# Matrix product with RMS norm on one core: a new order of steps, sums, squares and norms, and two row blocks loaded earlier

## The chip, the cores and the metric

The kernel runs on one core of one Trainium2 chip. The metric is the device time of one execution in microseconds (us). The kernel before has a median of 231.16 us over 3 runs (229.3 to 232.35). One further execution was profiled: it took 231.52 us, of which 229.7 us lie between its first and its last instruction (the span). All times of instructions below are counted from the start of that span.

A core has five engines that work side by side, each through its own queue in program order: PE (matrix products), DVE (vector work), ACT (activations, here squares, roots and copies), POOL (here almost only the loading of data) and SP (here only the issuing of output writes and of transposing transfers). They wait for each other through semaphores. Transfers between memories run on 16 DMA engines, which the loads from POOL and the transfers from SP share.

## The reference

```python
m, k, n = 2048, 2048, 2048          # a, b: randn float32; gamma: randn(n); eps = 1e-5
x = np.matmul(a, b)
rms = np.sqrt(np.mean(x ** 2, axis=-1, keepdims=True) + eps)
return (gamma * x / rms).astype(np.float32)
```

Every output row needs the whole row of x before it can be scaled, so squares are summed as chunks of the row come ready.

## The kernel before

**Tiling.** A has 16 row blocks of 128 rows (block 0 to 15), x has two column halves of 1024, each of two chunks of 512. Blocks 0 to 3 are the head; they are multiplied while B arrives. From block 4 on, two blocks make a group g (g = 2 to 7, rows `ra = 2g` and `rb = 2g + 1`). A group and a column half make a "half" n = 0 to 11, with g = 2 + n // 2 and j = n % 2.

**Products.** A half is computed as a 2 by 2 block product in Winograd's form of Strassen: seven products of 8 matmuls (128x512) each in place of eight. `do(n, m)` issues product m of half n and the copies of accumulators on ACT that belong to it; `take(n, what)` brings a finished chunk out (11 and 12 by ACT, 22 and 21 by an addition on DVE). `a_sums(g, which)` makes the sums of A's quarters on DVE that products 5, 6, 7 and 3 use. For groups 4 and 5, and for 6 and 7, product 2 (`a12*b21`) of the four halves together is replaced by a second level of the same scheme: `step(g, m, bank)` is one of its seven products of 4 matmuls; `a_two_sums(g)` makes its sums of A (in the tile x_5), `b_two(s)` those of B. Its results X2, W2 and Y2 (PSUM banks) are added into chunks of both groups by `add`.

**Row blocks of A.** A block is loaded as fp32 (1 MB) by POOL (`load_block`, L137) into one of two buffers of `a_pool`, so block m + 2 needs the buffer of block m. ACT takes its norm (`row_norm`, two squares and a root), DVE scales it to fp16 (`prepare`, L250, which calls `row_factor` and `row_apply`), and SP issues the transposing transfer into `at(m)` (L207 for blocks 6 to 9, L259 in two halves from block 10 on). A buffer of `a_pool` is free when both ACT's norm and DVE's scaling have read it. `at(m)` has four places: `at_even` and `at_odd`, two blocks each. `wait_for` is a POOL instruction that reads one element and so holds POOL's queue until that element is there; `load_after(src, mb)` is `wait_for(src)` and then `load_block(mb)`.

**Outputs.** `square_half` and `square_right` sum squares on ACT (the latter with the root); `finish` inverts on DVE, scales the two halves of a row block (2 x 1024 columns, gamma included) and lets SP write them.

**Order.** Every engine's order is written out by hand (`manual_schedule`): `first_segment` is n = 0; `segment(n)` is n = 1 to 9, of which n = 6 goes to `block_segment`; `last_group` is n = 10 and 11. Inside a segment the products of neighbouring halves alternate: half n's product 6, half n - 1's product 3, half n's product 2 (only before group 4), half n + 1's product 1, then n's products 7, 5 and 4. A PSUM bank that half n - 1 used (B3) must be read by `take(n - 1, 12)` or `take(n - 1, 22)` before the next product is put there.

**Where the blocks are loaded.** In the half with j = 1 of group g (`nxt = 2g + 2`), POOL waits for `at(nxt + 1)`, loads block nxt + 2, waits until it has landed and then loads nxt + 3 (L675, L676). So with g = 2 it is blocks 8 and 9, with g = 3 blocks 10 and 11, with g = 4 blocks 12 and 13, with g = 5 blocks 14 and 15. The norms of blocks 8 and 9 stand on ACT in segment n = 2 (L645 and L673).

Of the kernel before, what the change touches and what calls it, by code (L numbers as in the profile page):

```python
# [13 lines left out]
ALU = mybir.AluOpType  # L14
# [3 lines left out]
def kernel(  # L18
# [80 lines left out]
    def at(mb):  # L99
        return (at_even, at_odd)[(mb // 2) % 2][:, mb % 2]  # L100
# [4 lines left out]
    def add(out, in0, in1, op=ALU.add):  # L105
        nc.vector.tensor_tensor(out=out, in0=in0, in1=in1, op=op)  # L106
# [40 lines left out]
    def wait_for(src):  # L147
        nc.gpsimd.tensor_copy(out=pace, in_=src)
# [101 lines left out]
    def prepare(mb):  # L250
        row_factor(mb)
        if mb < 2 * (G2 + 1):
            row_apply(mb)
            transpose_dma(mb)
            return
        src, f = a32.pop(mb), factor.pop(mb)
        for h, dst in enumerate((a16_half, src.bitcast(FP16)[:, 0:HALF])):
            nc.vector.tensor_scalar_mul(out=dst, in0=src[:, h * HALF:(h + 1) * HALF], scalar1=f)
            nc.sync.dma_start_transpose(at(mb)[:, h * KP:(h + 1) * KP, :], dst)  # L259
# [24 lines left out]
    def square_half(mb, h):  # L284
        square_of(mb, x_tile(mb, h))
# [19 lines left out]
    def square_right(mb):  # L305

        square_half(mb, 1)
        rms_of[mb] = root(msq[mb][:, 2:3], pre_of.pop(mb))
# [28 lines left out]
    def a_sums(g, which, chained=True):  # L337
        a11, a12, a21, a22 = (quarter(g, r, c) for r in range(2) for c in range(2))
        terms = {3: (a22, sum_of(g, 2), ALU.subtract) if chained else (a11, a21, ALU.subtract),
                 1: (a21, a22, ALU.add),  # L340
                 2: (sum_of(g, 1), a11, ALU.subtract), 4: (a12, sum_of(g, 2), ALU.subtract)}
        for s in which:
            x, y, op = terms[s]
            nc.vector.tensor_tensor(out=sum_of(g, s), in0=x, in1=y, op=op)  # L344
# [45 lines left out]
    def a_two_sums(g):  # L390
        a11, a12, a21, a22 = (a_two(g, r, h) for r in range(2) for h in range(2))
        y1, y2, y3, y4 = (y_two[:, n] for n in range(4))
        add(y3, a11, a21, ALU.subtract)
        add(y1, a21, a22)
        add(y2, y1, a11, ALU.subtract)
        add(y4, a12, y2, ALU.subtract)
# [171 lines left out]
    def do(n, m, copies=True):  # L568

        if n >= len(halves) or n < 0:  # L570
            return
        g, j = halves[n]
        b1, b2, b3 = B1[n % 2], B2[n % 2], B3[n % 2]
        if g >= G2:
            b1 = b2
        product(g, j, m, {1: b1, 2: b1, 3: b3, 4: b2, 5: b3, 6: b2, 7: B7}[m],
                start=m in (1, 7))
        if m == 1 and g >= G2:
            nc.scalar.copy(out=chunks(n)[0], in_=b2)
        elif m == 1:  # L580
            nc.scalar.copy(out=b2, in_=b1)
        elif m == 6:
            nc.scalar.copy(out=b3, in_=b2)  # L583
        elif m == 7 and copies:
            nc.scalar.copy(out=chunks(n)[2], in_=B7)  # L585
# [13 lines left out]
    def load_after(src, mb):  # L599
        wait_for(src)  # L600
        load_block(mb)

    def first_segment():
        n, g, j = 0, G0, 0
        nxt = 2 * g + 2
        do(n, 1)
        do(n, 7, False)
        finish(0, (1,))
        pair_ends()
        do(n, 2)  # L610
        row_norm(nxt)
        a_sums(g, (4,))
        finish(0, (0,))
        do(n, 6)
        do(n + 1, 1)
        prepare(nxt)
        do(n, 5)
        nc.scalar.copy(out=chunks(n)[2], in_=B7)
        take(n, 22)
        row_norm(nxt + 1)  # L620
        take(n, 11)
        finish(1)
        do(n, 4)
        prepare(nxt + 1)
        take(n, 21)
        square_half(2 * g + 1, j)
# [7 lines left out]
    def segment(n):  # L634
        g, j = halves[n]
        ra, rb, nxt = 2 * g, 2 * g + 1, 2 * g + 2
        more = g + 1 < NG
        if g >= G2 and (g - G2) % 2 == 1 and j == 0:
            block_segment(n)
            return  # L640
        first = g >= G2 and (g - G2) % 2 == 0
        do(n, 6)
        if j == 0:
            finish(ra - 1)
            row_norm(nxt)  # L645
        elif g == G0:
            square_right(r2)
        do(n - 1, 3)
        take(n - 1, 12)
        if j == 0:  # L650
            square_right(ra - 2)
            prepare(nxt)
            a_sums(g, (4,))
            finish(ra - 2)
        else:
            if not first:
                square_half(ra, 0)
            if g == G0:
                square_right(r3)
                finish(r2, (1, 0))  # L660
            elif g == G2:
                b_two(4)
            elif not first and g > G2:
                finish(ra - 2)
        if g < G2:
            do(n, 2)
            take(n, 11)
        if g == G2 - 1 and j == 1:
            b_two(3)
            b_two(1)  # L670
        do(n + 1, 1)
        if j == 0:
            row_norm(nxt + 1)  # L673
        elif g + 2 < NG:
            load_after(at(nxt + 1)[:, KT - 1, 0:1], nxt + 2)  # L675
            load_after(a32[nxt + 2][:, 0:1], nxt + 3)  # L676
        if j == 1:
            a_sums(g + 1, (1, 2))
            if first:
                a_two_sums(g)  # L680
        do(n, 7)
        if j == 1:
            a_sums(g + 1, (3,))
        do(n, 5)
        take(n, 22)
        if j == 1:
            take_pre(rb)
            if not first:
                take_pre(ra)
        do(n, 4)  # L690
        take(n, 21)
        if j == 0:
            square_half(rb, 0)
            prepare(nxt + 1)
            if g == G2:
                b_two(2)
        else:
            square_right(rb)
            if g == G0:
                finish(r3, (1, 0))  # L700

    def block_segment(n):
        g, j = halves[n]
        ra, rb, nxt = 2 * g, 2 * g + 1, 2 * g + 2
        x00, x01, x10, x11 = first_sums(n)
        do(n, 6)
        finish(ra - 1)
        step(g - 1, 1, X2)
        nc.scalar.copy(out=W2, in_=X2)
        row_norm(nxt)  # L710
        do(n - 1, 3)
        step(g - 1, 2, W2)
        step(g - 1, 6, X2)
        nc.scalar.copy(out=Y2, in_=X2)
        take(n - 1, 12)
        add(x00, W2, x00)
        square_half(ra - 2, 0)
        prepare(nxt)
        do(n + 1, 1)
        step(g - 1, 5, Y2)  # L720
        step(g - 1, 7, W2)
        add(x11, Y2, x11)
        take_pre(ra - 2)
        row_norm(nxt + 1)
        a_sums(g, (4,))
        add(x10, W2, x10)
        add(x11, W2, x11)
        do(n, 7)
        step(g - 1, 4, X2)
        add(x10, X2, x10)  # L730
        do(n, 5)
        take(n, 22)
        step(g - 1, 3, Y2)
        add(x01, Y2, x01)
        square_right(ra - 2)
        prepare(nxt + 1)
        do(n, 4)
        take(n, 21)
        square_half(rb, 0)

    def last_group():
# [12 lines left out]
        def by_r(x, r):  # L754
# [2 lines left out]
        b2, b3 = [B2[(n + j) % 2] for j in range(2)], [B3[(n + j) % 2] for j in range(2)]  # L757
        x00, x01 = first_sums(n)[0:2]
        do(n, 6)
        finish(rb - 2)  # L760
        step(g - 1, 1, X2)
        nc.scalar.copy(out=W2, in_=X2)
        do(n - 1, 3)
        step(g - 1, 2, W2)
        step(g - 1, 6, X2)
        nc.scalar.copy(out=Y2, in_=X2)
        take(n - 1, 12)
        add(x00, W2, x00)
        square_half(ra - 2, 0)
        do(n + 1, 1)  # L770
        step(g - 1, 5, Y2)
        step(g - 1, 7, W2)
        add(x11[1], Y2, x11[1])
        take_pre(ra - 2)
        a_sums(g, (4,))
        add(x11[0], W2, x11[0])
        add(x11[1], W2, x11[1])
        square_of(ra, x11[1])
        do(n, 5)
        nc.scalar.copy(out=x22[0], in_=b3[0])  # L780
        step(g - 1, 4, X2)
        add(x11[0], X2, x11[0])
        do(n + 1, 6)
        step(g - 1, 3, Y2)
        add(x01, Y2, x01)
        square_right(ra - 2)
        do(n, 7)
        add(x22[0], x21[0], x22[0])
        add(b2[0], b2[0], x21[0])
        square_of(rb, x22[0])  # L790
        add(x11[1], x11[1], gam[2], ALU.mult)
        finish(ra - 2)
        do(n + 1, 5)
        nc.scalar.copy(out=x22[1], in_=b3[1])
        wide = a_pool.tile([P, K], FP32, name="a32")
# [4 lines left out]
        do(n, 3)  # L800
        take(n, 12)
        square_half(ra, 0)
        add(xa, xa, gam_left, ALU.mult)
        pre_a = stat_pool.tile([P, 1], FP32, name="pre")
        nc.vector.tensor_scalar(out=pre_a, in0=msq[ra][:, 0:1], scalar1=msq[ra][:, 1:2],
                                scalar2=msq[ra][:, 2:3], op0=ALU.add, op1=ALU.add)
        do(n + 1, 3)
        take(n + 1, 12)
        square_of(ra, x12[1])
# [84 lines left out]
```

## Time and profile before

| What | Value |
|---|---|
| Median of 3 runs | 231.16 us (229.3 to 232.35) |
| Profiled execution | 231.52 us, span 229.7 us |
| PE busy | 211.4 us, 92% of the span, 1004 matmuls |
| DVE busy | 161.7 us, 70% |
| ACT busy | 113.0 us, 49% |
| POOL busy | 37.0 us, 16% |
| Mean granted TensorE clock | 0.976 of full speed |
| Matmul 128x512, from one to the next, at full clock | 1.73 us for 8 |
| Load of a row block, issue to landing | 5.0 least, 5.4 median, 9.1 most (us, 10 loads) |
| Transposing transfer of a block (L207), issue to landing | 4.3 least, 4.3 median, 6.9 most (us, 4 transfers) |
| Output write of 512 KB, issue to landing | 3.6 median (us, 29 writes) |

How to read it: PE is busy for 92% of the span, and its 8% of pauses lie in a few places. A pause of PE counts fully if nothing that follows has slack to take it up. A row of the timeline gives the start, the busy time, the engine, the line of the code, the operation with its tiles, the number of instructions merged, and in brackets the idle time before it with the instruction that ended it. Matmuls overlap, so eight of them show 1.89 us busy though the next eight start 1.73 us later.

### The profile page before, as it was taken

How to read it: one execution, taken by the hardware profiler on the slowest of the kernel's cores; microseconds unless marked ns; L12 is line 12 of the kernel's file. 1: busy time of each engine (PE TensorE's matmuls, PEld its weight loads, DVE VectorE, ACT ScalarE, POOL GpSimd, SP SyncE). 2: the span in 40 equal slices, each digit the busy share in tenths (PEclk: the TensorE clock that was granted, in tenths of full speed). 3: DMA queues.
4: the chain of work that ended last, by engine and by line, in shares of the span. 5: the costliest groups of instructions: out<-in, count | busy, mean ns of one | idle time of the engine just before them, and what ended most of it. 6: DMA issues, size and time to landing. Idle time of an engine off the chain costs nothing.

```text
span 229.7 us, 2952 instructions
## 1 busy us (share of the span) xinstructions
PE 211.4 (92%) x1004; PEld 97.9 (43%) x1024; DVE 161.7 (70%) x323; ACT 113.0 (49%) x225; POOL 37.0 (16%) x74
## 2 busy tenths in 40 slices
PE   7999999999999999993799999999999999799960
PEld 3445454444454444441244444344444444344430
DVE  1237688999999858972853897687956956752981
ACT  2110004701987748574543972394738841445772
POOL 8544443342010002000011002100021000000030
PEclk9999999999999999999589999999999999999996
DMA  7999999999875695999254894488585972030255
GB/s 149 174 203 206 201 206 209 211 208 308 347 237 227 165 269 157 334 307 347 90 114 178 336 267 91 183 329 131 111 325 185 306 220 46 29 153 3 106 222 220
DMA packets 36911, 46.60 MB, mean 203 GB/s; under 512 B 22432, under 2 KB 26528, under 8 KB 35616
## 3 DMA queue, kind: packets, MB, share of 16 engines
q0 software_dynamic: 10608, 23.86, 42.8%
q1 hardware_dynamic: 26016, 22.29, 31.9%
q10 hardware_dynamic: 272, 0.26, 0.3%
q8 instruction: 8, 0.13, 0.2%
q14 instruction: 7, 0.06, 0.1%
HBM read 34.60 MB, written 16.78 MB: 224 GB/s over the span
## 4 chain that ended last, share of the span: by engine, by line
PE 33%; DVE 12%; DMA 7%; ACT 5%; issue 2%; SPq 1%; ACTq 0%; DVEq 0%
PE acc L367 28%; DVE x L106 5%; DMA a<-in_a_dram 4%; PE acc L406 3%; DVE x L320 3%; DMA head_at<-a 3%; DVE s L344 2%; ACT sq L281 2%; PE tbank L406 2%; ACT sq L229 1%; DVE head_at L344 1%; SPq L259 1%; DVE acc L106 1%; DVE a L106 1%; ACT rms L297 1%
## 5 line engine op out<-in xcount | busy, mean ns | idle before, releaser
L281 ACT ACTIVATE sq<-x 128x1024 bf16<-128x1024 f32 (+1 forms) x33 | 33.2, 1005 | 39.2 <-DVE x L106 35.9
L367 PEld LDWEIGHTS <-s 128*128 128x128 f16 (+1 forms) x312 | 30.7, 99 | 43.4 <-issue 7.3
L415 PE MATMUL acc<-b,head_at 128*128 128x512 bf16 x171 | 42.6, 380 | 0.2
L320 DVE SCALAR_TENSOR_TENSOR x<-x,r,gamma_sb 128x1024 f32<-128x1024 f32 x28 | 34.8, 1282 | 0.5
L367 PE MATMUL acc<-b,head_at 128*128 128x512 bf16 x133 | 34.8, 390 | 0.2
L106 DVE TENSOR_TENSOR x<-acc,x 128x512 f32<-128x512 f32 x33 | 22.6, 689 | 15.7 <-ACT x L585 5.1
L367 PE MATMUL acc<-b,s 128*128 128x512 bf16 x100 | 25.9, 399 | 5.2 <-DVE x L106 5.0
L229 ACT ACTIVATE sq<-a 128x1024 bf16<-128x1024 f32 x24 | 25.4, 1057 | 6.3 <-DMA a<-in_a_dram 5.9
L367 PEld LDWEIGHTS <-head_at 128*128 128x128 f16 (+1 forms) x184 | 18.2, 100 | 22.2 <-issue 2.2
L367 PE MATMUL acc<-b,at_even 128*128 128x512 bf16 x110 | 26.2, 379 | 0.2
L367 PE MATMUL acc<-early,s 128*128 128x512 bf16 x103 | 25.5, 379 | 0.1
L415 PEld LDWEIGHTS <-head_at 128*128 128x128 bf16 x176 | 17.0, 98 | 19.5 <-issue 0.9
L367 PEld LDWEIGHTS <-at_even 128*128 128x128 f16 x160 | 15.7, 98 | 18.9
L367 PE MATMUL acc<-t_left,s 128*128 128x512 bf16 x95 | 22.5, 379 | 0.0
L120 POOL DMA_DIRECT2D b<-in_b_dram x32 | 17.2, 540 | 20.6 <-DMA b<-in_b_dram 14.3
L451 ACT COPY x<-acc 128x512 f32<-128x512 f32 x7 | 4.1, 580 | 25.9 <-PE acc L415 25.9
L189 DVE COPY head_at<-tbank 128x1024 bf16<-128x1024 bf16 x7 | 4.8, 692 | 8.4 <-PE tbank L184 8.4
L106 DVE TENSOR_TENSOR x<-tbank,x 128x512 f32<-128x512 f32 x9 | 6.2, 692 | 4.8 <-PE tbank L441 3.6
L302 DVE RECIPROCAL r<-rms 128x1 f32<-128x1 f32 x16 | 2.5, 159 | 9.9 <-ACT rms L297 9.9
L820 POOL TENSOR_SCALAR x<-x,r 128x512 f32<-128x512 f32 x1 | 1.9, 1853 | 45.3 <-DVE r L302 45.3
L583 ACT COPY acc<-acc 128x512 f32<-128x512 f32 x12 | 6.9, 576 | 2.3 <-PE acc L367 2.3
L585 ACT COPY x<-acc 128x512 f32<-128x512 f32 x10 | 5.8, 576 | 4.6 <-PE acc L367 4.6
(129 smaller groups left out, 242.8 us busy)
## 6 DMA issues: line engine op xcount, KB each, us to landing
out_dram<-x SPq DMA_DIRECT2D x29, 512.0 KB, 3.6
a<-in_a_dram POOLq DMA_DIRECT2D x10, 1024.0 KB, 5.4
b<-in_b_dram POOLq DMA_DIRECT2D x32, 256.0 KB, 9.9
a<-in_a_dram POOLq DMA_DIRECT2D x4, 512.0 KB, 9.8
early<-in_a_dram POOLq DMA_DIRECT2D x7, 256.0 KB, 10.3
gamma_sb<-in_gamma_dram POOLq DMA_DIRECT2D x2, 512.0 KB, 9.9
out_dram<-x SPq DMA_DIRECT2D x3, 256.0 KB, 2.6
out_dram<-a SPq DMA_DIRECT2D x1, 768.0 KB, 3.3
```

What stands on the lines that cost most here:

```text
L106: nc.vector.tensor_tensor(out=out, in0=in0, in1=in1, op=op)
L120: nc.gpsimd.dma_start(out=raw[j][kp][:, t, :], in_=b[lo:lo + P, j * HALF:(j + 1) * HALF])
L189: nc.vector.tensor_copy(out=head_at[:, 2 * kp:2 * kp + 2, :, :], in_=view)
L229: nc.scalar.activation(out=junk, in_=a32[mb][:, h * HALF:(h + 1) * HALF], func=ACTF.Square, scale=2.0 ** -8, accum_out=n2[:, h:h + 1])
L281: nc.scalar.activation(out=sq[:, 0:src.shape[-1]], in_=src, func=ACTF.Square, scale=inv_sqrt_n, accum_out=msq[mb][:, c:c + 1])
L320: nc.vector.scalar_tensor_tensor(out=x, in0=x, scalar=inverse_of[mb], in1=gamma_sb[:, h * HALF:(h + 1) * HALF], op0=ALU.mult, op1=ALU.mult)
L344: nc.vector.tensor_tensor(out=sum_of(g, s), in0=x, in1=y, op=op)
L367: nc.tensor.matmul(bank, lhsT[:, kp, :], rhs, start=(start and kp == 0), stop=(kp == KP - 1), skip_group_check=not start)
L406: nc.tensor.matmul(bank, lhsT[:, k, :], rhs, start=(m in (1, 7) and k == 0), stop=(k == KQ - 1), skip_group_check=m not in (1, 7))
L415: nc.tensor.matmul(bank, head_at[:, kt, r, :], head_rhs(c, kt), start=(kt == 0), stop=(kt == KT - 1))
L583: nc.scalar.copy(out=b3, in_=b2)
L585: nc.scalar.copy(out=chunks(n)[2], in_=B7)
```

## The change

Two loads are moved forward: block 8 is loaded from `first_segment`, right after `prepare(6)`, and block 10 from segment n = 2, right after `prepare(8)`; POOL then waits for `at(7)` before block 9, and for `at(9)` before block 11. From group 4 on, loading is as before. In the j = 1 halves of groups 4 and 6 (n = 5 and 9), `a_two_sums` stands before `a_sums(g + 1, (1, 2))`, and `square_right(rb)` leaves the end of the segment: it now stands in `block_segment` and `last_group` behind the first copy of X2 to W2. In these two, `finish` of that row comes two steps later, step 4 is issued right behind step 7, step 3 before `do(n, 5)` in `block_segment`, norms and preparations of the next blocks come later, and in `last_group` some squares, one `finish` and one small sum of squares (`pre_a`) come in another order.

```diff
@@ first_segment
         prepare(nxt)
+        load_block(nxt + 2)
         do(n, 5)
@@ segment
         if j == 0:
             square_right(ra - 2)
             prepare(nxt)
+            if g < G2:
+                load_block(nxt + 2)
             a_sums(g, (4,))
             finish(ra - 2)
...
         elif g + 2 < NG:
-            load_after(at(nxt + 1)[:, KT - 1, 0:1], nxt + 2)
-            load_after(a32[nxt + 2][:, 0:1], nxt + 3)
+            wait_for(at(nxt + 1)[:, KT - 1, 0:1])
+            if g >= G2:
+                load_block(nxt + 2)
+                wait_for(a32[nxt + 2][:, 0:1])
+            load_block(nxt + 3)
         if j == 1:
-            a_sums(g + 1, (1, 2))
             if first:
                 a_two_sums(g)
+            a_sums(g + 1, (1, 2))
...
-            square_right(rb)
+            if not first:
+                square_right(rb)
@@ block_segment
         do(n, 6)
-        finish(ra - 1)
         step(g - 1, 1, X2)
         nc.scalar.copy(out=W2, in_=X2)
-        row_norm(nxt)
+        square_right(ra - 1)
         do(n - 1, 3)
         step(g - 1, 2, W2)
         step(g - 1, 6, X2)
         nc.scalar.copy(out=Y2, in_=X2)
+        finish(ra - 1)
         take(n - 1, 12)
         add(x00, W2, x00)
-        square_half(ra - 2, 0)
-        prepare(nxt)
         do(n + 1, 1)
         step(g - 1, 5, Y2)
         step(g - 1, 7, W2)
+        step(g - 1, 4, X2)
+        square_half(ra - 2, 0)
+        row_norm(nxt)
         add(x11, Y2, x11)
-        take_pre(ra - 2)
-        row_norm(nxt + 1)
         a_sums(g, (4,))
         add(x10, W2, x10)
         add(x11, W2, x11)
+        take_pre(ra - 2)
         do(n, 7)
-        step(g - 1, 4, X2)
+        row_norm(nxt + 1)
         add(x10, X2, x10)
+        prepare(nxt)
+        step(g - 1, 3, Y2)
         do(n, 5)
         take(n, 22)
-        step(g - 1, 3, Y2)
         add(x01, Y2, x01)
         square_right(ra - 2)
-        prepare(nxt + 1)
         do(n, 4)
         take(n, 21)
+        prepare(nxt + 1)
         square_half(rb, 0)
@@ last_group
         do(n, 6)
-        finish(rb - 2)
         step(g - 1, 1, X2)
         nc.scalar.copy(out=W2, in_=X2)
+        square_right(rb - 2)
         do(n - 1, 3)
         step(g - 1, 2, W2)
         step(g - 1, 6, X2)
         nc.scalar.copy(out=Y2, in_=X2)
+        finish(rb - 2)
         take(n - 1, 12)
         add(x00, W2, x00)
-        square_half(ra - 2, 0)
         do(n + 1, 1)
         step(g - 1, 5, Y2)
         step(g - 1, 7, W2)
+        step(g - 1, 4, X2)
+        square_half(ra - 2, 0)
         add(x11[1], Y2, x11[1])
-        take_pre(ra - 2)
         a_sums(g, (4,))
         add(x11[0], W2, x11[0])
         add(x11[1], W2, x11[1])
+        take_pre(ra - 2)
         square_of(ra, x11[1])
         do(n, 5)
         nc.scalar.copy(out=x22[0], in_=b3[0])
-        step(g - 1, 4, X2)
         add(x11[0], X2, x11[0])
-        do(n + 1, 6)
         step(g - 1, 3, Y2)
         add(x01, Y2, x01)
         square_right(ra - 2)
+        do(n + 1, 6)
+        finish(ra - 2)
         do(n, 7)
...
         add(x11[1], x11[1], gam[2], ALU.mult)
-        finish(ra - 2)
         do(n + 1, 5)
...
         square_half(ra, 0)
-        add(xa, xa, gam_left, ALU.mult)
         pre_a = stat_pool.tile([P, 1], FP32, name="pre")
         nc.vector.tensor_scalar(out=pre_a, in0=msq[ra][:, 0:1], scalar1=msq[ra][:, 1:2],
                                 scalar2=msq[ra][:, 2:3], op0=ALU.add, op1=ALU.add)
+        add(xa, xa, gam_left, ALU.mult)
```

Each engine executes as many instructions as before, except POOL, which has two waits (`wait_for`) fewer.

## The prediction

> **What bounds the kernel now.** I read the page's shares first: PE is busy for 92% of the span, no other engine for more than 70%. So only PE's pauses, and what follows its last matmul, can be won. The slices show where they lie: PE falls to 3 and 7 in slices 19 and 20, and PEclk, the granted clock, falls with it.
>
> ```profile
> PE   7999999999999999993799999999999999799960
> PEclk9999999999999999999589999999999999999996
> ```
>
> The timeline of PE gives the size of each pause (start, busy time, bracket: idle before and what ended it):
>
> ```profile
> 103.53 1.89 PE L367 MATMUL acc<-early,s 128*128 128x512 bf16 x8
> 110.42 3.57 PE L367 MATMUL acc<-b,s 128*128 128x512 bf16 x8 [5.00 <-DVE x L106]
> 113.78 3.08 PE L367 MATMUL acc<-b,head_at 128*128 128x512 bf16 x8
> 116.70 1.89 PE L367 MATMUL acc<-b,at_even 128*128 128x512 bf16 x8
> ...
> 146.92 1.89 PE L367 MATMUL acc<-b,s 128*128 128x512 bf16 x8
> 149.84 1.02 PE L406 MATMUL acc<-b,at_even 128*128 128x512 bf16 x4 [1.03 <-ACT acc L709]
> ...
> 195.94 1.89 PE L367 MATMUL acc<-b,s 128*128 128x512 bf16 x7
> 199.27 1.02 PE L406 MATMUL acc<-b,at_even 128*128 128x512 bf16 x4 [1.44 <-ACT acc L762]
> ```
>
> The big pause is followed by two products at half speed; the windows view shows the clock (after the five busy columns: PEclk, DMA share, GB/s):
>
> ```profile
> 109.00:111.00 2.00, 0.58 (x2) 0.25 (x2) 1.22 (x2) 0.64 (x2) 0.00 (x0) 0.59 0.57 231
> 111.00:113.00 2.00, 2.00 (x7) 0.65 (x5) 1.90 (x7) 1.63 (x3) 0.00 (x0) 0.50 0.00 0
> 113.00:115.00 2.00, 2.00 (x6) 0.67 (x5) 1.94 (x7) 0.94 (x2) 0.00 (x0) 0.50 0.36 72
> 115.00:117.00 2.00, 2.00 (x8) 0.81 (x7) 1.16 (x3) 0.89 (x3) 0.00 (x0) 0.70 1.03 191
> ```
>
> Last the chain of waits (start, length, what), read from the transfer down: block 9's load lands at 106.49, ACT takes its norm, only then copies B7 (L585), DVE does take(2, 22), and PE may write that bank.
>
> ```profile
> 97.36 9.13 DMA a<-in_a_dram
> 106.49 0.02 issue
> 106.51 1.16 ACT sq L229 x2
> ...
> 109.08 0.57 ACT x L585
> 109.65 0.02 issue
> 109.67 0.70 DVE x L106
> ```
>
> The same view leads the two pauses at 149.84 and 199.27 back through ACT's copies (L709, L762) to square_right of the row before: its squares and root stand before them in ACT's queue and wait for DVE's take(21), which is late because a_sums and a_two_sums start only when block 11 (or 15) is transposed (142.10, 191.53).
>
> **Early loads: the gain.** POOL's queue stands at its wait for at(7) from 66.9 to 87.4 us, so load 8 now goes out once DVE has scaled block 6, at 77.1 (before: 88.23). Block 9 needs only at(7) and goes out near 89 in place of 97.36; with the 9.13 us that load took among other traffic it lands by about 98. ACT reaches norm 9 earlier too: norm 8 starts behind the copy that ends at 95.0, not at 96.70, so norm 9 starts at about 100.5, B7 is copied by 103.6, take(2, 22) is done by 104.4. PE is ready at 103.53 + 1.73 = 105.26 (8 matmuls start 1.73 apart in every undisturbed row). So the pause of 110.42 - 105.26 = 5.16 us goes. With it goes the slow clock: 116.70 - 110.42 = 6.28 us for two products, 2.82 over 2 x 1.73. Together **-7.98 us**. Next late is take(2, 22) itself, with 0.9 us to spare.
>
> A rule bears on the second term. The row is 2.82 us. The Trainium skill (TensorE: Matmul & The Clock Gate, "What's actually happening") says that an idle window of about 3.4 us halves the clock and a busy one of 3.4 us restores it; an estimate from that page alone would be 1.7 us lost, and a sum 1.1 us smaller. I keep the row.
>
> **Early loads: the cost.** Load 8 now runs beside the transposing transfer of block 6 (issued 77.19) and the writes at 80.00. PE needs at(6) at 84.53, in product 1 of half 2. Rows: at(9), alone, landed 4.3 us after issue; at(8), with load 9 beside it for 5 us, 6.9 us, and SP was held for 4.82 us, not 1.93. By 4.3 at(6) lands at 81.5, by 6.9 at 84.1: no cost. If it had to wait for a whole load of 9.13 first, 77.19 + 9.13 + 4.3 = 90.6: 6.1 us of pause and 2.8 of slow clock. I take **+0.5**, near the 6.9 row, but load 8 lies beside all of it. SP's writes and at(7) slip behind; at(7) landed at 87.4 and PE needs its sums at 91.44, two DVE operations (1.5 us) after landing, so 2.5 us are covered. Load 10 meets at(8) likewise: prepare(8) ends near 100.2, 6.9 more is 107.1, PE needs it at 105.26 + 2 x 1.73 = 108.7: nothing, with 1.6 us to spare. Loads 10 and 11 are wanted by ACT 5 us or more after they land (ACT took norms 10 and 11 at 126.50 and 131.50, so some 8 us before that now). POOL's two dropped waits free only POOL.
>
> A rule of the Trainium skill speaks against this part: DMA: Bandwidth & Descriptors, "Queues, rings and completion order", has each DMA engine take turns between queues packet by packet. At half rate the alone row doubles to 8.6 us as an estimate, at(6) lands at 85.8, and the cost would be 1.3, not 0.5.
>
> **Steps, squares, norms.** Moving a_two_sums forward: it reads blocks 8 and 10 only, and DVE is idle for 1.21 us (4.65 at the second place) before block 11 (15) lands, so its 1.6 us end at about 142.6, and the sum for product 6 is ready at 144.1 where PE wants it at 144.33: 0.2 us to spare. Moving square_right behind the copy to W2: the copy is then ready at 147.5, and PE needs it at 146.92 + 1.73 = 148.65, so 149.84 - 148.65 = **-1.19 us**. Next late is step 7: finish now stands before add(x00, W2): root 149.2, reciprocal and two 1.28 us scalings to 151.9, addition to 152.5; PE comes to step 7 at 152.97. 0.4 us to spare; with step 4 behind it, the bank of step 3 is added long before.
>
> Norms and preparations of 12 and 13 come later. By ACT's and DVE's durations (a norm 2.56 us, a preparation 2.3) norm 12 ends at 156.5 and at(12) is issued near 159.6 instead of 155.50, landing about 162.9; PE wants it at 164.2: covered. at(13) lands 0.4 us later than its 167.1, hence loads 14 and 15 too: block 15 lands near 179.3 + 0.4 (issue 173.93 plus the median 5.4), while ACT, now 1.19 ahead, wants it at 180.17 - 1.19 = 179.0. That 0.7 us passes through L585, take(8, 22) and prepare(15) to at(15), which already was the last thing product 6 of half 10 waited for (193.15 against 193.01). I give back **+0.6**.
>
> In the last group three pauses go: 195.94 - 195.75 = 0.19, 199.27 - 197.67 = 1.60, and 220.57 - 219.99 = 0.58, before the last two half products, which waited for DVE. There finish of row 12 (2.48 us) and the multiplication of xa (1.2 us) stood before pre_a and the inverse (219.49); with finish done by 211 and pre_a first, the inverse comes near 216.7 and the bank additions by 217.7, PE being ready at 218.2. **-2.37 us**, if the tail behind it (root, last scalings, writes) moves whole.
>
> **Sum.** -7.98 + 0.5 - 1.19 + 0.6 - 2.37 = -10.44. The profiled execution took 231.52, 1.82 more than its span and 0.36 over the median: 231.52 - 10.44 = **221.1 us**.
>
> **Rivals.**
> - *Transposes held up*: each of at(6) and at(8) late by 1 to 2 us (twice the 4.3 row), at(7) and load 9 with them. For: DMA share is already 1.17 at 79 to 81 us. Against: at(8) beside load 9 came in 6.9. Price 2 to 4: 223 to 225.
> - *The new order gives nothing*: finish before step 7, or the late norms, make a pause as long as the one removed. For: only 0.2 and 0.4 us to spare. Against: each row computed above. Without the 0.6 and the 2.37: about 224.
> - *Slower*: a transfer of POOL's, once queued, is finished before the transposing one beside it. Then at(6) costs 6.1 + 2.8 = 8.9, and at(8), at 100.2 + 13.4 = 113.6 against 108.7, another 4.9 + 2.8: 16.6 against gains of 10.9, 231.5 + 5.7 = 237. It decides once at(6) and at(8) together cost more than 10.9. Against: behind load 9, at(8) landed at 108.3, not 106.49 + 4.3 = 110.8.
> - *Load 8 does not go earlier*: no, the order listing has it ahead of POOL's wait, and DVE's scaling of block 6 is its last condition. At most the steps' part would be left (-1.19 + 0.6 - 2.37): 228.6.
>
> **How the numbers follow.** Forecast 0.64, held transposes 0.18, order without gain 0.08, load not earlier 0.02, slower 0.05, and a mixture that eats all 0.03. Two per cent (4.6 us) is about what a measurement of this kernel tells from no change, so faster means below 226.5. Forecast and the first two rivals lie below it: 0.90; the fourth and the mixture between: 0.05; slower 0.05. Range: down to the gains without any give-back (231.5 - 11.5 = 220.0) less 1.2 for the spread of the runs, 218.8; up to the held transposes, 225.0.
>
> **What would show it.** Right: no pause of PE near 105, clock 1.00 there, load 8 out near 77, load 9 near 89, ACT not waiting for a transfer before norms 8 and 9; W2's copy (now L715, L769) before square_right, and no pause ahead of step 2. Wrong: a pause at product 1 of half 2 or 4 ended by a transposing transfer, a pause at step 7 ended by DVE, or product 6 of half 10 waiting longer for at(15).

## The result and the profile after

The changed kernel takes 238.51 us, the median of 4 runs (237.75 to 239.57). The kernel before took 231.28 us on the same chip (4 runs, 229.3 to 232.35). The ratio is 1.033 (95%: 1.024 to 1.041): slower, where 221.1 us had been forecast. The profiled execution took 237.75 us, with a span of 236.0 us and a mean granted clock of 0.959 (before: 0.976).

The slices of the page after, to be read against those of before:

```profile
PE   7799999999999931999999999999999579999970
PEclk9999999999999985799999999999999958999997
```

The hole of before in slices 19 and 20 is closed. In its place there is a larger one in slices 15 and 16, and a new one in slices 32 and 33, each with the slow clock behind it. The timeline of PE says what ended them (start, busy time, bracket: idle before and what ended it):

```profile
82.69 1.89 PE L367 MATMUL acc<-b,at_even 128*128 128x512 bf16 x8
93.39 3.59 PE L367 MATMUL acc<-b,head_at 128*128 128x512 bf16 x8 [8.82 <-DMA head_at<-head_at]
96.78 1.97 PE L367 MATMUL acc<-early,s 128*128 128x512 bf16 x8
98.59 1.89 PE L367 MATMUL acc<-b,at_even 128*128 128x512 bf16 x8
...
149.53 1.89 PE L367 MATMUL acc<-b,s 128*128 128x512 bf16 x8
151.25 1.03 PE L406 MATMUL acc<-b,at_even 128*128 128x512 bf16 x4
...
184.06 1.89 PE L367 MATMUL acc<-early,s 128*128 128x512 bf16 x8
190.18 2.29 PE L367 MATMUL acc<-b,s 128*128 128x512 bf16 x5 [4.23 <-DVE x L106]
...
196.45 1.89 PE L367 MATMUL acc<-early,s 128*128 128x512 bf16 x8
...
204.22 1.89 PE L367 MATMUL acc<-b,s 128*128 128x512 bf16 x7
205.95 1.03 PE L406 MATMUL acc<-b,at_even 128*128 128x512 bf16 x4
```

The first hole is product 1 of half 2, which waits for `at(6)`: 93.39 - (82.69 + 1.73) = 8.97 us of pause, and (98.59 - 93.39) - 2 x 1.73 = 1.74 us lost to the slow clock, **+10.71** together. The second is product 3 of half 8: 190.18 - (184.06 + 1.73) = 4.39 us, and (196.45 - 190.18) - 2 x 1.73 = 2.81 us, **+7.20**. No product between 98.59 and 190.18 shows a wait in its row: the 7.98 us of before near 105 are gone. The rows at 151.25 and 205.95 have no bracket any more, so the pauses ahead of step 2 are gone too.

The chain of waits names the transfers behind both holes (start, length, what):

```profile
77.06 16.28 DMA head_at<-head_at
...
171.54 5.26 DMA a<-in_a_dram
177.66 8.59 DMA a<-in_a_dram
186.28 1.16 ACT sq L229 x2
...
190.18 2.29 PE acc L367 x5
```

The transposing transfer of block 6 took 16.28 us where the same transfer took 4.3 alone. Block 15's load took 8.59 us where 5.5 had been enough before, and ACT's norm of block 15, with the copy of B7 behind it, stood until it landed.

The windows view shows what the DMA engines did in the first hole (after five busy columns: PEclk, DMA share, GB/s):

```profile
80.00:82.00 2.00, 2.00 (x11) 0.88 (x9) 1.90 (x6) 0.09 (x1) 0.00 (x0) 1.00 1.97 147
82.00:84.00 2.00, 2.00 (x11) 0.90 (x10) 1.54 (x2) 0.43 (x1) 0.00 (x0) 1.00 0.84 91
...
90.00:92.00 2.00, 0.00 (x0) 0.00 (x0) 0.00 (x0) 0.00 (x0) 0.00 (x0) 0.50 0.75 102
```

Their share is no lower than before (1.11 and 0.73 from 80 to 84), but they move 147 and 91 GB/s in these two stretches, where before they moved 328 and 297. Engines that are as busy with a third to a half of the bytes: packets are in flight and stand. I call this the crawl.

The sum of all differences is -7.98 + 10.71 - 1.19 + 7.20 - 2.37 = +6.37; 231.52 + 6.37 = 237.89 us, and 237.75 were measured.

### The profile page after: what moved, and what is told of

Read it like the earlier page. It is cut to its first block, busy times and chain, and to the rows that moved or that the text cites. A ratio compares the mean times of both kernels' runs of the same rounds, so it can differ in the third digit from the quotient of the medians.

```text
span 236.0 us, 2950 instructions
## 1 busy us (share of the span) xinstructions
PE 211.4 (90%) x1004; PEld 97.9 (41%) x1024; DVE 161.6 (68%) x323; ACT 114.3 (48%) x225; POOL 36.9 (16%) x72
## 4 chain that ended last, share of the span: by engine, by line
PE 72%; DMA 17%; ACT 3%; issue 2%; DVE 2%; POOL 1%; ACTq 0%; another core or an unknown queue 0%; SPq 0%; POOLq 0%
PE acc L367 48%; PE acc L415 15%; DMA head_at<-head_at 7%; DMA a<-in_a_dram 6%; PE acc L406 3%; DMA early<-in_a_dram 3%; PE tbank L406 2%; PE tbank L441 2%; DMA at_even<-a 2%; PE tbank L184 1%; ACT sq L229 1%; PE tbank L367 1%; DVE x L106 1%; PE tbank L197 0%; POOL b L120 0%
## 5 line engine op out<-in xcount | busy, mean ns | idle before, releaser
L367 PE MATMUL acc<-b,head_at 128*128 128x512 bf16 x133 | 36.5, 405 | 9.0 <-DMA head_at<-head_at 8.8
L415 PE MATMUL acc<-b,head_at 128*128 128x512 bf16 x171 | 42.3, 379 | 1.4 <-DMA b<-in_b_dram 1.2
L415 PEld LDWEIGHTS <-head_at 128*128 128x128 bf16 x176 | 16.9, 98 | 20.4 <-issue 1.3
L451 ACT COPY x<-acc 128x512 f32<-128x512 f32 x7 | 4.1, 581 | 25.6 <-PE acc L415 25.6
L139 POOL DMA_DIRECT2D a<-in_a_dram x10 | 5.3, 531 | 34.4 <-ACT acc L581 11.8
L344 DVE TENSOR_TENSOR head_at<-head_at 128x1024 f16<-128x1024 f16 (+1 forms) x4 | 2.8, 688 | 10.7 <-DMA head_at<-head_at 8.2
```

The lines of the kernel that those rows point to most:

```text
L139: nc.gpsimd.dma_start(out=a32[mb], in_=a[mb * P:(mb + 1) * P, :])
L367: nc.tensor.matmul(bank, lhsT[:, kp, :], rhs, start=(start and kp == 0), stop=(kp == KP - 1), skip_group_check=not start)
L415: nc.tensor.matmul(bank, head_at[:, kt, r, :], head_rhs(c, kt), start=(kt == 0), stop=(kt == KT - 1))
```

## The experiments

**Each half of the change alone.** The first kernel is the one before with only the early loads; the second is the changed one with the loading of before.

```diff
@@ e1_loads (against before): first_segment; segment
         prepare(nxt)
+        load_block(nxt + 2)
...
+            if g < G2:
+                load_block(nxt + 2)
...
-            load_after(at(nxt + 1)[:, KT - 1, 0:1], nxt + 2)
-            load_after(a32[nxt + 2][:, 0:1], nxt + 3)
+            wait_for(at(nxt + 1)[:, KT - 1, 0:1])
+            if g >= G2:
+                load_block(nxt + 2)
+                wait_for(a32[nxt + 2][:, 0:1])
+            load_block(nxt + 3)
@@ e2_steps (against after): the same lines taken back
```

> The kernel before with the two early loads alone, all steps, squares and norms in the old order. Theory (collision: a block's load that comes up while a transposing transfer is under way makes both crawl): block 6's transfer takes some 16 us as in the changed kernel, PE pauses about 9 us at product 1 of half 2 and runs slowly for 1.7 more, the old pause at 105 us (7.98 with its slow clock) is gone: 231.3 + 10.7 - 8.0 = 234.0 us, with the small pauses at the two second-level groups back and no pause ahead of half 9. Rival (the order of the steps is what costs, the loads pay on balance): below 231.

> The changed kernel with the old loading, so the new order of steps, squares and norms alone. Theory (collision): the later preparations of blocks 12 and 13 push load 15 into block 14's transposing transfer; that load takes about 8.6 us and PE pauses 4.4 us plus 2.8 of slow clock ahead of product 3 of half 8: 231.3 - 1.2 - 2.4 + 7.2 = 234.9 us, and the pause at 105 us stays. Rival (as forecast, the late loads cost 0.6 us only and the second pause of the changed kernel came from the early loads): 228.3 us.

The early loads alone took 236.24 us, a ratio of 1.020 (1.013 to 1.028), where 234.0 us had been expected. The timeline of PE has the first hole and not the second:

```profile
95.48 3.29 PE L367 MATMUL acc<-b,head_at 128*128 128x512 bf16 x8 [10.11 <-DMA head_at<-head_at]
```

Block 6's transfer took 17.6 us and load 8 took 16.9 us. The new order alone took 233.21 us, a ratio of 1.005 (1.000 to 1.010), and has the second hole beside the old pause at 105:

```profile
110.27 3.57 PE L367 MATMUL acc<-b,s 128*128 128x512 bf16 x8 [4.84 <-DVE x L106]
187.37 3.56 PE L367 MATMUL acc<-b,s 128*128 128x512 bf16 x8 [4.33 <-DVE x L106]
```

So the first hole belongs to the early loads, and the second to the new order and not to them. The size of the second kernel's loss was smaller than expected: 233.8 us in its profiled execution, 0.5% in the runs.

**The pair without a wait.** In before, block 9's load goes right behind block 8's, and nothing else changes.

```diff
@@ e3_pair (against before): segment
-            load_after(at(nxt + 1)[:, KT - 1, 0:1], nxt + 2)
-            load_after(a32[nxt + 2][:, 0:1], nxt + 3)
+            wait_for(at(nxt + 1)[:, KT - 1, 0:1])
+            load_block(nxt + 2)
+            if g > G0:
+                wait_for(a32[nxt + 2][:, 0:1])
+            load_block(nxt + 3)
```

> The kernel before, but POOL loads block 9 right behind block 8, without waiting for block 8 to land (blocks 11, 13, 15 still wait). Nothing of these loads lies beside a transposing transfer: both come after block 7 is turned and should land before block 8's transfer begins near 100 us. Theory (collision): block 9 lands by about 99, its norm is not waited for, the pause at 105 and the slow clock go: 231.3 - 8.0 = 223.3 us, and block 8's transfer, with no load beside it, lands in some 4.3 us and not 6.9. Rival (the loads are held by the six output writes of that time, whatever the order): block 9 lands near 104, about half of the pause stays, 227 us.

It took 227.92 us, a ratio of 0.982 (0.974 to 0.990). The pause at 105 shrank from 5.00 to 0.87 us of idle time, so block 9 needs no early block 8: the wait between the two loads was nearly its whole cause. Two new pauses took part of the gain back, 1.64 us (at 131.34) and 1.30 us (at 181.79). There ACT waited for loads 11 and 15, which still waited for their partners; they landed at 127.41 and 177.86, after 6.8 and 6.7 us. Neither line of reasoning had these. One sign failed: block 8's transfer was to land in 4.3 us with no load beside it, and took 7.3. Load 9's last packet had passed by 101.3; what went ahead of the transfer, from 101.4 to 103.7, were some 230 packets of output writes in its own queue.

**Load 8 held back until the transfer is done.** POOL reads an element of `at(6)` before it issues load 8.

```diff
@@ e4_hold (against after): first_segment
         prepare(nxt)
+        wait_for(at(nxt)[:, KT - 1, 0:1])
         load_block(nxt + 2)
```

> The changed kernel, but POOL waits for block 6 to be turned before it loads block 8. The load then meets block 7's transposing transfer (issued near 83 us), not block 6's. Theory (collision): block 6's transfer takes about 4.3 us again and the pause at product 1 of half 2 goes; now block 7's transfer crawls (over 10 us) and PE pauses at product 6 of half 2, its sums of A waiting: about 236 us. Rival (the output writes of row block 1, issued between the two transfers, hold block 6's transfer, not the load): block 6's transfer still takes over 10 us, and the time stays at 238.5.

It took 227.55 us, a ratio of 0.983 (0.977 to 0.989). Block 6's transfer was back at 4.4 us. PE's timeline has no hole at product 1 of half 2 and still the one in half 8:

```profile
84.94 1.89 PE L367 MATMUL acc<-b,head_at 128*128 128x512 bf16 x8
...
180.95 3.57 PE L367 MATMUL acc<-b,s 128*128 128x512 bf16 x8 [4.12 <-DVE x L106]
```

With 5 us more of waiting the early load is a gain. But my first form of the theory fell here: load 8 now ran into block 7's transfer (issue 83.54), which should have crawled as well. It took only 7.3 us, and the load 6.5. So a load beside a transfer does not suffice for the crawl. The packet counts, below, show what goes with it.

**Are the output writes part of it?** In this kernel the two writes of row block 1, which lie between the transfers of blocks 6 and 7, are left out; so that part of the output is missing.

```diff
@@ e5_nowrite (against after): finish; first_segment
-            nc.sync.dma_start(out=rows(mb, h * HALF, (h + 1) * HALF), in_=x)
+            if write:
+                nc.sync.dma_start(out=rows(mb, h * HALF, (h + 1) * HALF), in_=x)
...
-        finish(1)
+        finish(1, write=False)
```

> The changed kernel without the two output writes of row block 1 (1 MB, not written at all), which SP issues 2.8 us after block 6's transposing transfer and whose packets come while load 8 and that transfer are under way. Theory (the load and the transposing transfer alone are enough): block 6's transfer still takes over 10 us and PE still pauses some 9 us at product 1 of half 2; time near 238. Rival (the three together, the writes queued behind the transposing transfer on SP's ring, make the crawl): block 6's transfer lands within 8.5 us as block 8's does, the pause is under 1.5 us, and the time falls by 8 to 10 us.

One execution took 248.13 us, beside 231.21 before. Block 6's transfer took 17.0 us with no write near it, and block 8's now crawled too, with 17.6 us. The timeline of PE:

```profile
94.07 3.60 PE L368 MATMUL acc<-b,head_at 128*128 128x512 bf16 x8 [9.57 <-DMA head_at<-head_at]
...
129.12 3.60 PE L368 MATMUL acc<-b,at_even 128*128 128x512 bf16 x8 [8.35 <-DMA at_even<-head_at]
```

The rival that wants the writes fell. That block 8's transfer crawls here and not in after is the best hint: load 10's first packet now came when 1,201 of the transfer's packets had moved, in after when 1,852 had.

**The packets.** The view of the DMA queues counts packets (queue, kind: packets, MB, share of 16 engines); q1 holds SP's transfers, q0 POOL's loads. A transfer of a block moves as 2,048 packets of 256 B, a load as 128 of 8 KB, an output write in packets of 4 KB; each also has a few of 4 B. After, from 78 to 79, from 79 to 80, and from 80 to 92 us:

```profile
q1 hardware_dynamic: 445, 0.11, 60.2%
...
q1 hardware_dynamic: 664, 0.17, 107.8%
q0 software_dynamic: 2, 0.02, 3.9%
...
DMA packets 1136, 1.42 MB, mean 118 GB/s; under 512 B 973, under 2 KB 973, under 8 KB 1011
q1 hardware_dynamic: 996, 0.39, 60.7%
q0 software_dynamic: 140, 1.02, 50.5%
```

The load's first packet comes at 79.98, when 1,101 of the transfer's packets have moved. The rest, which at 664 in a us would need 1.4 us, then take over 12, and the load's packets as long. The same view of before, for load 9 and block 8's transfer, from 101 to 105 and from 105 to 108 us:

```profile
DMA packets 241, 1.31 MB, mean 328 GB/s; under 512 B 32, under 2 KB 32, under 8 KB 131
q0 software_dynamic: 115, 0.90, 61.1%
...
DMA packets 2154, 0.84 MB, mean 281 GB/s; under 512 B 2082, under 2 KB 2082, under 8 KB 2147
```

Here the load was ahead. For 4 us the transfer moved at most 32 packets, and then all of its own within 3 us. But 99 of the 241 packets (131 - 32) are output writes, which stand ahead of the transfer in SP's queue, so this row alone does not say whether it waited for the load or for them. Held back (e4_hold), block 7's transfer shows it without writes, from 84 to 88 and from 88 to 90 us:

```profile
q0 software_dynamic: 120, 0.98, 88.0%
q1 hardware_dynamic: 2, 0.00, 0.0%
...
q1 hardware_dynamic: 1821, 0.47, 109.8%
```

While the load moved 120 packets, the transfer's queue moved 2: it waited, it did not share. In e6_actq, below, it is the same from 79 to 82 us: 94 packets of the load, none of SP's queue.

So there are three cases by the moment at which the load's first packet comes. Ahead of the transfer's: the transfer waits for the load and takes 7.3 to 8.0 us (e4_hold, c1_hold_pair, e6_actq, e10_actmid). When about half has moved (1,101 packets in after, 1,126 in e1_loads, 1,115 and 1,201 in e5_nowrite): both crawl, and the transfer takes 16.3 to 17.6 us. Near the end (1,852 at block 8's transfer in after, 1,794 to 1,861 in all nine kernels where it meets an early load 10 and does not crawl): a tail, 8.4 to 9.0 us. No run has a load come between the first packet and 1,101, or between 1,201 and 1,794, so where one case ends and the next begins is not known. The moment of issue does not set the case: in after, loads 8 and 10 both went out 0.5 us behind the transfer, and their first packets came 2.4 and 3.6 us later. Why, no run shows.

**Moving the moment.** If this holds, a load issued a few us earlier or later does not crawl. These kernels move load 8 alone, everything else as in after: in all five the line `load_block(nxt + 2)` behind `prepare(nxt)` goes, where ACT issues, `load_block` is given the queue, and in e10 and e11 `row_norm(7)` is given the block (these lines are not shown).

```diff
@@ e6_actq: first_segment, issued by ACT, ahead of the transfer's packets
-        load_block(nxt + 2)
         do(n, 5)
         nc.scalar.copy(out=chunks(n)[2], in_=B7)
+        load_block(nxt + 2, nc.scalar)
@@ e7_actlate: first_segment, issued by ACT
         row_norm(nxt + 1)
+        load_block(nxt + 2, nc.scalar)
@@ e8_norm: first_segment, issued by POOL after norm 7
         row_norm(nxt + 1)
+        wait_for(norm[nxt + 1])
+        load_block(nxt + 2)
@@ e10_actmid: row_norm(7), issued by ACT between the two squares
         for h in range(2):
+            if h == 1 and between is not None:
+                load_block(between, nc.scalar)
@@ e11_actmid2: row_norm(7), issued by ACT behind them, ahead of the root
+        if then is not None:
+            load_block(then, nc.scalar)
         norm[mb] = stat_pool.tile([P, 1], FP32, name="norm")
```

> The changed kernel with load 8 issued from ACT's queue (behind the copy of B7, near 77 us) and not from POOL's; everything else the same. Theory (any 1 MB load that comes up inside the transposing transfer): the crawl stays, block 6's transfer over 10 us, time near 238. Rival (POOL's own way of issuing makes the load's packets slow): the load runs at its full rate, block 6's transfer lands within 8.5 us and the pause at product 1 of half 2 goes.

> The changed kernel with load 8 on ACT's queue, but behind norm 7 (issue near 79.4 us), so that its packets come up near 80 us, when about half of block 6's transposing transfer has moved, as POOL's load does in the changed kernel. Theory (what counts is that a load comes up in the middle of the transfer, whoever issues it): block 6's transfer takes over 12 us, PE pauses 8 us or more at product 1 of half 2, time near 238. Rival (only loads issued by POOL crawl there): the load runs through in some 4 us, block 6's transfer lands by 86, the pause stays under 2 us, time near 229.

> The changed kernel with load 8 still issued by POOL, but some 2.5 us later, behind a wait for norm 7, so that its packets come up when block 6's transfer has all but moved. Theory (what counts is how much of the transfer is left): no crawl, block 6's transfer lands in 4.3 to 5 us, the load is over before block 7's transfer has been waited for, the pause at product 1 of half 2 goes and only the one at 181 us stays: about 227 us. Rival (any load within the transfers of blocks 6 and 7 crawls): block 7's transfer takes over 12 us and PE pauses over 5 us at product 6 of half 2; over 233.

> As the run with load 8 on ACT's queue behind norm 7, but between that norm's two squares (issue near 78.3 us), so that its packets come near 79.7 us, in the middle of block 6's transposing transfer; in the earlier run they came at 81.1, when the transfer had all but moved, and nothing was told apart. Theory (a load that comes up in the middle crawls, whoever issues it): block 6's transfer over 12 us, PE pauses 8 us or more at product 1 of half 2, time near 238. Rival (only POOL's loads crawl): the load and the transfer are both through by 87 us, the pause is under 3 us, time near 229.

> As before with load 8 on ACT's queue, now behind both squares of norm 7 and ahead of its root, so issued between 78.2 and 79.1 us and with packets near 79.8 us, in the middle of block 6's transposing transfer (the two earlier placings came 1 us before it and after nine tenths of it). Theory (a load that comes up in the middle crawls, whoever issues it): block 6's transfer over 12 us, PE pauses 8 us or more at product 1 of half 2, time near 238. Rival (only POOL's loads crawl there): load and transfer are both through by 87 us, the pause is under 3 us, time near 229.

The kernel that decides whether the delay is enough is e8_norm, with POOL's own queue: its load went out at 80.28 instead of 77.53, only 2.75 us later, and took 8.3 us. Its first packet came at 83.17, when block 6's transfer had landed (4.3 us) and ahead of block 7's, which took 7.4 us. Time 227.59 us, a ratio of 0.983 (0.977 to 0.990). From 80 to 92 us its queues moved, against after's 1.42 MB:

```profile
DMA packets 3559, 3.75 MB, mean 313 GB/s; under 512 B 2947, under 2 KB 2947, under 8 KB 3431
```

With ACT's queue there are four kernels of one execution each, none with a crawl. In e6_actq (228.03 us) and e10_actmid (227.88) the load's packets came first: the load took 6.2 and 5.9 us, the transfer waited and took 8.0 and 7.7. In e7_actlate (227.51) they came when 2,009 packets had moved, in e11_actmid2 (228.62) when 1,932 had: the transfer took 4.6 and 8.5 us. Both e10_actmid and e11_actmid2 were aimed at the middle and missed it. In e10_actmid ACT issued its load at 77.01, while the square before it still ran. So these four agree with the three cases, but whether a load from another queue than POOL's would crawl in the middle stays open.

**Versions that should beat both.** One kernel takes e4_hold and also drops the wait between the loads of a pair in groups 4 and 5. One takes the new order, with no early load, and every pair back to back behind `at(nxt + 1)`. The third does that to the kernel before.

```diff
@@ c1_hold_pair (against e4_hold): segment
-                wait_for(a32[nxt + 2][:, 0:1])
@@ c2_pairs (against e2_steps), e9_pairs_old (against before): segment
-            load_after(at(nxt + 1)[:, KT - 1, 0:1], nxt + 2)
-            load_after(a32[nxt + 2][:, 0:1], nxt + 3)
+            wait_for(at(nxt + 1)[:, KT - 1, 0:1])
+            load_block(nxt + 2)
+            load_block(nxt + 3)
```

> The changed kernel with load 8 held until block 6 is turned (as in the run before), and with loads 13 and 15 issued right behind 12 and 14, without waiting for those to land. Theory (collision): load 15 is over before block 14's transposing transfer begins, so the pause of 4.1 us ahead of product 3 of half 8 and its 2.8 us of slow clock go: about 7 us less than the 227.55 of the kernel with the hold alone, 220.6 us. Rival (the late norms and preparations of blocks 12 and 13 make that pause): it stays, 227.5.

> The new order of steps, squares and norms, no early load, and every pair of blocks loaded back to back once the block before them is turned. Theory (collision): no load lies beside a transposing transfer any more; the pause at 105 us shrinks to about 0.9, those of 149 and 199 go and the one at 186 does not come: 232.4 (the kernel before on this chip) less 7.1, 1.2 and 2.4, 221.7 us. Rival (two loads at once delay the first of the pair, whose norm comes first): new waits of ACT for blocks 10, 12 or 14, above 225.

> The kernel before with every pair of blocks loaded back to back and all steps, squares and norms in the old order: what the pairs alone are worth. Theory: 231.2 less the pause at 105 us and its slow clock, 7.1 to 8.0, so 223.2 to 224.1 us, and the difference to the same loads in the new order (220.26) is the worth of the steps, 3.0 to 3.6 us. Rival (the old order hides part of its own pauses once the loads are early, or load pairs bring new ones): 226 or more, or under 222.

They took 221.05 us (ratio 0.956, 0.951 to 0.961), 220.26 us (0.952, 0.948 to 0.957) and 223.41 us (0.965, 0.959 to 0.972). With c1_hold_pair the pause in half 8 is gone: the wait between loads 14 and 15 was needed for it. c2_pairs is the fastest kernel of the study, and its slices have no hole:

```profile
PE   7799999999999999999999999999999999999960
PEclk9999999999999999999999999999999999999997
```

The same loading with the old order keeps the pauses ahead of step 2 (1.05 and 1.26 us, at 142.32 and 191.22), so the new order is worth 0.965 - 0.952 = 1.3%, some 3 us, once the loads do not stand in its way. The rest of the gain is the one wait that is dropped for each pair.

## Why the prediction was wrong

**The bound** was read rightly: only PE's pauses and the slow clock behind them count, and the account of them closes within 0.2 us.

**The gains came, but the changed kernel does not test the largest.** The -7.98 near 105 is gone from it. Yet load 9 went out at 98.24 and not near 89, because `at(7)` was itself late, and PE came to that product at 115.86, 10.6 us later than forecast, which alone is more than the pause of 5.16. So that row alone does not tell the forecast from luck. The forecast mechanism shows in e8_norm: load 9 goes out at 91.18 and lands at 96.63, and no product near 105 has a wait in its row. The -1.19 came (149.53 + 1.73 = 151.26, and step 2 starts at 151.25), and so did the -2.37 of the last group (204.22 + 1.73 = 205.95, and step 2 of `last_group` starts there); in e2_steps, with the new order alone, these waits are gone too. The thin spares held: step 7 and the sum for product 6 show no pause.

**The failed step is the +0.5 for the cost of the early loads.** It was taken near the 6.9 us row of block 8's transfer, read as the price of a transfer that runs beside a load. The packets show that hardly anything ran side by side in that row: the transfer's packets came when the load and the writes ahead of it had all but moved. So the row spoke rather for the bound that I set aside, a transfer that waits for the load (90.6). And even that bound was too low: `at(6)` landed at 77.06 + 16.28 = 93.34. No row of before shows the two meeting in the middle, so the bounds were drawn from one side only. The term is 10.71, 10.2 more than forecast.

The Trainium skill (DMA: Bandwidth & Descriptors, "Queues, rings and completion order") has each DMA engine take turns between its queues packet by packet. The tail of block 8's transfer in the changed kernel agrees with it, from 114.5 to 117 us:

```profile
q0 software_dynamic: 94, 0.77, 94.8%
q1 hardware_dynamic: 87, 0.02, 6.3%
```

That is one packet of the transfer for one of the load, but 256 B against 8 KB. So turns by packet do not halve the transfer's rate, as the prediction's estimate of 8.6 us had it; block 8's transfer took 8.6 us by another way, with nine tenths of it moved before the load came. The other two cases are not such turns: a transfer behind a load moved next to nothing, and in the crawl, at 16.3 to 17.6 us, both were slow. Here the measurement decides.

**Mis-sized is the +0.6 for late loads 14 and 15: it measured 7.20.** The chain was named rightly as far as take(8, 22) (at(13), load 14, load 15, norm 15, L585), and e2_steps shows that it comes from the order alone. The prediction led it on to at(15) and product 6 of half 10, but PE already stopped at product 3 of half 8, whose bank take(8, 22) frees; product 6 of half 10 has no wait. Two sizes were off. `at(13)` was to be 0.4 us later; it landed at 170.78, 3.77 later than before, with PE itself 1.4 later by then, so some 2.3 belong to the order. And load 15 was given the median of 5.4 us; it took 8.59 in its later place, beside two output writes. SP's and POOL's timelines:

```profile
177.70 1.53 SPq L323 DMA_DIRECT2D out_dram<-x  x2
181.03 1.87 SPq L259 DMA_TRANSPOSE head_at<-a_half  x1
183.10 4.20 SPq L259 DMA_TRANSPOSE head_at<-a  x1
```

```profile
176.93 0.79 POOL L148 COPY pace<-a 128x1 f32<-128x1 f32 x1 [4.85 <-DMA a<-in_a_dram]
177.66 0.53 POOL L139 DMA_DIRECT2D a<-in_a_dram  x1
```

Load 15 goes out only when load 14 has landed. Its first packet comes 2.9 us after issue (in before 1.25), when the first write has moved; the queues from 178.5 to 180.5, from 180.5 to 183.5 and from 183.5 to 185 us:

```profile
q1 hardware_dynamic: 136, 0.52, 89.0%
...
q0 software_dynamic: 98, 0.80, 85.2%
...
q1 hardware_dynamic: 82, 0.31, 51.4%
q0 software_dynamic: 39, 0.22, 38.2%
```

From 183.5 the second write shares the engines with it. Block 14's transfers move no data before 184.9, so it is these writes that lie beside the load. The median of a transfer is the price of its old neighbours; a moved transfer has new ones.

**The cost of load 10 at block 8's transfer** was forecast at nothing. In after PE did not wait for it, though the transfer took 8.6 us: it landed at 118.64, and PE, by then some 10 us later than forecast, wanted it at 119.31. In e4_hold it cost 0.31 us of idle time, which is near the forecast; but e5_nowrite, with 8.35 us, shows that this was a matter of timing and not of spare time.

**The rivals.** "Slower" gave 237 us, and its number is nearly the measured one, by other terms. It wanted 8.9 us at `at(6)` and 7.7 at `at(8)`, by finishing the load first. Measured are 10.71 from the crawl, nothing at `at(8)`, and 7.20 in half 8, which it did not have. A load that is finished first cost little: in e6_actq PE paused 0.56 us. "Transposes held up" had the right place, at a price of 2 to 4 us against 10.71. The sign that was to prove the forecast wrong, a pause at product 1 of half 2 ended by a transposing transfer, is the very row at 93.39.

**The clock.** After 8.97 us of pause 1.74 us were lost to the slow clock, after 4.39 us 2.81, and before 2.82 after 5.16. From the windows of about 3.4 us in the Trainium skill (TensorE: Matmul & The Clock Gate, "What's actually happening") the prediction had an estimate of 1.7; it fits the first and not the others. The granted clock was 0.50 in these stretches, two of the changed kernel and one of before:

```profile
86.70:96.93 10.23, 3.54 (x9) 1.33 (x10) 2.59 (x3) 3.56 (x7) 0.00 (x0) 0.50 1.05 202
189.10:195.92 6.82, 5.52 (x13) 2.08 (x14) 4.91 (x12) 2.52 (x5) 0.00 (x0) 0.50 0.70 203
...
109.37:116.19 6.82, 5.77 (x14) 2.02 (x14) 6.21 (x15) 3.64 (x7) 0.00 (x0) 0.50 0.43 107
```

PE resumed at 93.39, 190.18 and 110.42, so 3.5, 5.7 and 5.8 us of the slow stretch fell on its products, and half of that is about the loss. So in these three what counts is how much of the slow stretch is left when PE resumes, and not how long it paused. What sets the length of the stretch, no run shows.

## What to carry to other kernels

Before a load is moved, list the transposing transfers in flight when its first packet will come, and price the meeting as a wait for the whole other transfer, or worse; a row that looks like two transfers side by side should be split into packets by time before it is used as a price. When the cause of a late transfer is a wait between two loads, drop that wait before moving anything: here `wait_for` on block 8 was all but 0.9 us of the pause at 105, and its removal for every pair gave 3.5% without a new order. After a gain upstream, look again at each transfer that keeps its wait, for it meets other neighbours than before.

## What the runs showed of the hardware

- A load of 1 MB and a transposing transfer of a block do not share the DMA engines evenly. A load whose packets come first holds the transfer's back (120 packets against 2 in 4 us, e4_hold). If the load's first packet comes when 1,101 to 1,201 of the transfer's 2,048 have moved, both take 15.6 to 17.6 us instead of 5.4 and 4.3, at 118 GB/s in all from 80 to 92 us of the changed kernel. This was seen at four meetings in three kernels, all with loads from POOL's queue. Why it happens is not shown.
- A crawling transfer holds SP's queue. SP's issue of block 7's transfer lasted 12.49 us, where it lasted 1.71 in before, as its timeline in the changed kernel shows:

```profile
77.06 2.08 SPq L207 DMA_TRANSPOSE head_at<-head_at  x1
79.88 1.58 SPq L323 DMA_DIRECT2D out_dram<-x  x2
83.02 12.49 SPq L207 DMA_TRANSPOSE head_at<-head_at  x1
```

- Two loads of 1 MB issued back to back did not delay the first: in c2_pairs loads 8, 10, 12 and 14 took 7.5, 5.1, 5.1 and 5.2 us, in before 8.4, 5.1, 5.0 and 5.5.
